# Layer 1's compression pages requested behind the output products of layer 0's attention

## The chip, the core and the metric

The kernel runs on one core of a Trainium2 chip. The metric is device time in microseconds (us); a kernel's time is the median of its runs. Its engines are TensorE (PE, with the weight loads PEld beside it), VectorE (DVE), ScalarE (ACT), GpSimd (POOL) and SyncE (SP). In this kernel SP issues every DMA, and the transfers run on the core's 16 DMA engines.

## The reference, cut to what matters

A decoder step of two layers over 512 prompt tokens and 8 x 4 sample tokens, 1024 channels wide. Each layer normalises its input and multiplies it with one wide weight matrix. The columns feed a state-space branch (S5), an attention branch (NSA) and two sets of merge gates. Both branches are projected to 1024 channels, weighted by the gates, summed, multiplied with an output matrix and added to the layer's input:

```
kc = compress_rows(kv_all[:, :, 0], cmp_pe[0], cmp_w1[0], cmp_w2[0])
vc = compress_rows(kv_all[:, :, 1], cmp_pe[1], cmp_w1[1], cmp_w2[1])
...
b_nsa = (o * jax.nn.silu(z_nsa)) @ lp['w_nsa_out']
m_s5, m_nsa = jnp.split(jax.nn.sigmoid(merge_logits), 2, axis=-1)
out = (m_s5 * b_s5 + m_nsa * b_nsa) @ lp['w_o']
x = x + gate[:, None] * out
```

`compress_rows` turns every block of 64 cached key or value rows into one row by a small two-step network. The cached rows lie in pages of 128 rows, which a page table scatters over a pool. Each layer reads all 128 pages (8 samples x 16 pages) for its compression. That part depends on the cache and on nothing that the previous layer computes.

## The kernel before, in words

Activations are held feature-major: channel blocks of 128 on the partitions, all 544 tokens in the free dimension, worked on in two halves of 256 and 288 tokens. Matrix products in `mm` (line 490) are done in two-part arithmetic: each operand is split into a high and a low part, and three products are summed. A block of output channels times a half of the tokens is 24 matmuls where the contraction is 1024 deep and 12 where it is 512 deep.

**Who sets the order.** The program is written as generators that run against a model clock while the kernel is built (`_Sched.run`, line 252). Each generator emits instructions and yields: `ev` waits until another generator has called `done` with that name, `t` waits some model time, `for` waits for data by the model's clock. A smaller priority number goes first among those that are ready. So the order in which instructions stand in each engine's program, SP's DMA requests too, is fixed when the kernel is built; on the chip every engine works through its own list in that order. Nearly every instruction has the same source line in the profile (the recording helper, line 231), so tiles are told apart by name: `in_cmp` are the compression pages, `mn` and `mt` the spilled gates, `in_nsaow` and `in_wo` the attention's output weights and the layer's output weights, `in_ada_w` the modulation weights. Buffers of the on-chip arena are all called `m`, PSUM banks `bank`.

**Output products of the attention** (in `dense`, lines 1090 to 1122; called the gates' stage below). For each of 8 blocks m of output channels and each token half h: 12 matmuls with `in_nsaow`, then DVE multiplies the sum with the gate `mn`, adds the S5 branch `mt`, and the result is split into two parts. `mn` and `mt` were spilled to DRAM earlier; `gates(m)` (line 1090) reads both back, 272 KB each, into a ring of three buffers, two blocks ahead. Behind the loop stand 8 blocks of products with `in_wo` (the output stage), 24 matmuls a half, beside which the layer's input `in_xT` is loaded and the new activation `x_mid` stored. The weights of all products are requested two blocks of 512 KB ahead of use (`wnext`, line 465).

**Compression of the next layer** (`compress`, line 1612). It is spawned once layer 0's attention is done (event `att`), so it runs beside the gates' stage and the output stage. It loads its first weight (`in_cw`, two halves of 1024 KB) and a position tile (`in_pe`, twice 128 KB), and spawns `loads` (line 1639). `loads` requests 8 chunks of 16 pages, 128 KB a page, four pages at a time, each four behind SP's reading of their page numbers. Layer 1 has two page buffers, so chunk c waits for the products of chunk c - 2 (event `ck`). The products of a chunk are 64 matmul pairs, emitted as 128 matmuls with 64 output rows, ahead of the dense products because their priority number is smaller. Chunks 0 to 4 may come as soon as their pages are there by the model's clock; chunk 5 and later wait until layer 0 is finished (`CMP_LATE`), and the last waits for layer 1's own new rows.

**Modulation of layer 1** (`modulation`, line 531) starts at the same event: 24 blocks of `in_ada_w`, 512 KB each, two at a time, 8 blocks for each of three parts; parts 0 and 1 scale and shift layer 1's input, so `modulate(1)` (line 671) needs them, together with the row norms, before layer 1's first product.

Of the kernel before, what the change touches and what calls it, by code (L numbers as in the profile page):

```python
# [292 lines left out]
def body(ctx: ExitStack, tc: tile.TileContext, A, O):  # L293
# [52 lines left out]
    def t(lat=0.0):  # L346
        return ("t", lat)
# [3 lines left out]
    def ev(*k):  # L351
        return ("ev", k)

    def done(*k):
        S.events[k] = S.ready

    def alloc(n, top=False, keep=0):
        while not mem.fits(n, keep):
            yield "mem", n, keep
        return mem.get(n, top)  # L360
# [150 lines left out]
    def sub(dst_lo, src, hi):  # L511
        dve.tensor_tensor(dst_lo, src, hi.bitcast(F32), op=ALU.subtract)
# [13 lines left out]
    def unlag():  # L526
        while lagged:
            sub(*lagged.pop())
# [226 lines left out]
    def dense(l):  # L755
# [352 lines left out]
        for m2 in range(4):  # L1108
            w = wnext(("nsaow", l, m2))
            for m in (2 * m2, 2 * m2 + 1):  # L1110
# [3 lines left out]
                for h, (a, b) in enumerate(HALVES):  # L1114
# [5 lines left out]
                    split_lag(mh(m, a, b), ml(m, a, b), mt(m, a, b))  # L1120
                    yield t()
        unlag()
        for b in mnb:
            b.free()
        for b in q["ogh"] + [q["ogb"]]:
# [440 lines left out]
    def page_ids(i, n=4):  # L1566
        S.clock.free["sp"] = max(S.clock.free.get("sp", 0.0), S.now) + 0.3 + 0.11 * n
        _, v = nc.values_load_multi_w_load_instructions(
            pt[0:1, i:i + n], engines=[mybir.EngineType.SP], min_val=0, max_val=A["cmp"].shape[0] - 1,
            skip_runtime_bounds_check_because="the page table is clamped to the pool on chip")  # L1570
        return v


    def hidden(hid, b, n, th, xb):

        v = lambda t_: t_[:, 0:2 * n].rearrange("p (n g) -> p g n", g=2)
        dve.scalar_tensor_tensor(hid[:, b, :, 0:n], v(th), 1.0, v(xb), op0=ALU.add, op1=ALU.mult)

    def keys(dst, tmp, cw2, hid, b0, n, w, bank):

        vps = bank[:, 0:w * n].rearrange("p (b n) -> p b n", b=n)
        sh = [P, n, w]
        for j in range(2):
            for g in range(2):
                pe.matmul(bank[g * 64:g * 64 + 64, 0:w * n], cw2[0:64, j, :], hid[0:64, b0:b0 + n, g, 0:w],
                          start=True, stop=True)
            dve.tensor_tensor(dst if j == 0 else tmp, vps,
                              C["kcC" if j == 0 else "kcS"][:, None, 0:w].to_broadcast(sh), op=ALU.mult)
            yield w_
        dve.tensor_tensor(dst, dst, tmp, op=ALU.add)  # L1590
        dve.tensor_scalar(dst, dst, 0.5, None, op0=ALU.mult)

    def products(ck, cw1, npx, bank):
        for d in range(32):
            for ty in range(2):
                pe.matmul(bank[ty * 64:ty * 64 + 64, 0:npx * 4], cw1[ty][:, d, :], ck[:, 0:npx, ty, d, :],
                          start=(d == 0), stop=(d == 31))
            if d % PROD_STEP == PROD_STEP - 1:
                yield t(PROD_GAP)

    def compressed_of(l):

        q = L[l]
        if "kcb" not in q:
            q["kcb"] = None
            kcb = q["kcb"] = yield from alloc(8 * 32 + 2 * P + 16 + 512 + 1 + 128)
            q["kcT"], q["vc"], q["cw2"] = kcb.v(8, 32), kcb.v(2, P, at=256), kcb.v(2, 64, at=1041)
            sp.dma_start(q["cw2"], A["cw2"][l])
            done("kcb", l)
        yield ev("kcb", l)  # L1610

    def compress(l):

        q, keep = L[l], CMP_KEEP if l else 0
        yield from compressed_of(l)
        kcT, vc, cw2, pbias = q["kcT"], q["vc"], q["cw2"], q["kcb"].v(1, at=1040)
        kcbd, vcbd = q["kcbd"], q["vcbd"] = q["kcb"].v(2, 8, at=512), q["kcb"].v(8, 64, p=64, at=528)
        cwb = []
        for _ in range(2):
            cwb.append((yield from alloc(2048, True, keep)))  # L1620
        cw1 = [b.v(32, 64) for b in cwb]

        ckb = []
        for _ in range(CKB[l]):
            ckb.append((yield from alloc((NPG + 5) * 256, True, keep)))
        cks = [b.v(NPG + 5, 2, 32, 4) for b in ckb]
        hb = yield from alloc(512 + 256 + 84 * 2 + 64 + 8 * 2 + 64 * 2, True, keep)
        hid, kt1 = hb.v(8, 2, 32), hb.v(8, 32, at=512)
        xb, th = hb.v(84, at=768), hb.v(84, at=852)
        hnew, kc, kt2, hrep, vcr = (hb.v(1, 2, 32, at=936), hb.v(1, 8, at=1000), hb.v(1, 8, at=1008),  # L1630
                                    hb.v(4, 2, 8, at=1016), hb.v(64, p=64, at=1080))
        for ty in range(2):
            sp.dma_start(cw1[ty], A["cw1"][l, :, ty])
        for ck in cks:
            sp.dma_start(ck[:, NPG].rearrange("p t d c -> p (t d c)"), A["pe4"][l])
        q["cpage"] = cks[(NB - 1) % CKB[l]][:, NPG + 1:NPG + 5]
        done("ckb", l)

        def loads():
            for c in range(NB):  # L1640
                if c >= CKB[l]:
                    yield ev("ck", l, c - CKB[l])
                ck = cks[c % CKB[l]]
                for i in range(0, NPG, 4):
                    for j, v in enumerate(page_ids(NPG * c + i)):
                        sp.dma_start(ck[:, i + j].rearrange("p t d c -> p (t d c)"),
                                     A["cmp"][ds(v, 1), l].rearrange("g p f -> (g p) f"))
                    yield t(PG_LAT)
                yield "for", [], [ck[:, 0:NPG + 1]]
                yield t(CK_LATE)  # L1650
                done("ckl", l, c)
        S.spawn(loads(), 4, "ckload")
        if l > 0:
            yield ev("att", l - 1)
        for c in range(NB):
            if l > 0 and c == CMP_LATE:
                yield ev("x", l - 1)
            last = c == NB - 1
            if last:
                yield ev("cp", l)  # L1660
            yield ev("ckl", l, c)
            npx = NPG + 5 if last else NPG + (c == 0)
            if last:
                yield "for", [], [cks[c % CKB[l]][:, NPG + 1:]]
            yield from products(cks[c % CKB[l]], cw1, npx, B[7])
            done("ck", l, c)
            for b in ([ckb[c % CKB[l]]] if c + CKB[l] >= NB else []) + (cwb if last else []):
                b.free()
            if c == 0:
                dve.tensor_copy(pbias, B[7][:, 64:65])  # L1670
            n = 84 if last else 64
            dve.tensor_scalar(xb[:, 0:n], B[7][:, 0:n], pbias, None, op0=ALU.add)
            act.activation(th[:, 0:n], xb[:, 0:n], AF.Tanh, scale=0.5)
            if last:
                hidden(hnew, 0, 8, th[:, 68:84], xb[:, 68:84])
            hidden(hid, c, 32, th, xb)
        yield w_

        yield from keys(kc, kt2, cw2, hnew, 0, 1, 8, B[7])
        pool.memset(kcbd, 0.0)  # L1680
        for g in range(2):
            dve.tensor_copy(kcbd[g * 64:g * 64 + 64, g, :], kc[g * 64:g * 64 + 64, 0, :])
        dve.tensor_copy(hrep, hnew[:, 0:1, :, 0:8].to_broadcast([P, 4, 2, 8]))
        yield w_
        pe.matmul(B[7][0:64, 0:64], hrep[64:128].rearrange("p r g n -> p (r g n)"), cw2[64:128, 0, :],
                  start=True, stop=True)
        act.activation(vcr, B[7][0:64, 0:64], AF.Copy, scale=0.5)
        dve.tensor_tensor(vcbd, vcr[:, None, :].to_broadcast([64, 8, 64]),
                          C["bd8"][0:64, :, None].to_broadcast([64, 8, 64]), op=ALU.mult)
        done("kcbd", l)  # L1690
        yield w_

        yield from keys(kcT, kt1, cw2, hid, 0, 8, 32, B[7])
        for bh in range(2):
            for b in range(4):
                for g in range(2):
                    pe.matmul(B[7][32 * b:32 * b + 32, g * 64:g * 64 + 64], hid[64:128, 4 * bh + b, g, :],
                              cw2[64:128, 0, :], start=True, stop=True)
            act.activation(vc[:, bh, :], B[7][:, 0:P], AF.Copy, scale=0.5)
            yield w_  # L1700
        hb.free()
        done("cmp", l)
# [385 lines left out]
    def main():  # L2088
# [4 lines left out]
        S.spawn(modulation_first([B[6], B[4]]), 2, "ada0")  # L2093
        S.spawn(modulate(0), 3, "h")
        S.spawn(dense(0), 50, "dense")
        yield ev("modq", 0)
        sp.dma_start(pt, A["page_table"])
# [256 lines left out]
```

## Time and profile before

| | us |
|---|---|
| median of three runs | 1247.3 |
| lowest and highest run | 1238.85, 1257.79 |
| the profiled execution | 1244.75 |
| its span | 1243.0 |
| PE busy in the span | 1142.0 (92%) |
| DVE busy | 780.4 (63%) |
| ACT busy | 481.5 (39%) |

The profiled execution is 1.75 us longer than its span; that much lies around the recorded instructions. Rows of the trace give a start in us from the span's begin, a duration, the engine, the operation with its tiles, a count, and in brackets the engine's idle time before it with the one that ended it. A row merges neighbours of one engine and group, and shows the first one's shape.

### The profile page before, as it was taken

To read this page: it belongs to the slowest core of one execution; us is meant where nothing else is said; L and a number is where in the kernel's file an instruction comes from. 1 tells how busy PE (TensorE), PEld (TensorE's weight loads), DVE (VectorE), ACT (ScalarE), POOL (GpSimd) and SP (SyncE) were. 2 spreads that over 40 slices of the span, in tenths; PEclk is the share of its full clock that TensorE was granted. 3 is DMA by queue.
4 is the path that set the end of the run, shared out by engine and by line. 5 is a ranking of instruction groups with operands and counts; after the bars stand their busy time and mean duration, and the time that the engine had idled before them with its cause. 6 is when DMAs were issued, how large, how long until landed. Compare 5 with 4: busy or idle time off the path is not lost.

```text
span 1243.0 us, 30351 instructions
## 1 busy us (share of the span) xinstructions
PE 1142.0 (92%) x11702; PEld 1037.6 (83%) x11702; DVE 780.4 (63%) x1787; ACT 481.5 (39%) x1130; POOL 154.8 (12%) x335
## 2 busy tenths in 40 slices
PE   4989999999999999887897999979999899999995
PEld 3788999988888888777885899868898788889995
DVE  4766777566666755763336587797665667556854
ACT  4432432333444444432125233244343444454332
POOL 0122261010000000000002033450010000000001
PEclk9999999999999999988998999989999999999997
DMA  9575666657567655349998744545466665733742
GB/s 386 218 225 180 192 181 187 180 176 245 153 187 237 190 165 170 107 165 294 308 308 262 268 162 133 160 135 142 129 213 197 197 194 167 235 104 97 237 131 81
DMA packets 174434, 239.19 MB, mean 192 GB/s; under 512 B 33233, under 2 KB 129618, under 8 KB 172498
## 3 DMA queue, kind: packets, MB, share of 16 engines
q1 hardware_dynamic: 174290, 237.25, 60.2%
q8 instruction: 92, 1.51, 0.5%
q14 instruction: 52, 0.43, 0.1%
HBM read 207.53 MB, written 37.98 MB: 198 GB/s over the span
## 4 chain that ended last, share of the span: by engine, by line
PE 69%; DMA 11%; DVE 7%; ACT 4%; SPq 4%; issue 2%; POOL 0%; DVEq 0%; ACTq 0%; POOLq 0%
PE bank L231 69%; DVE m L231 7%; SPq L231 3%; ACT m L231 3%; DMA m<-in_cmp 2%; DMA m<-in_cw 2%; DMA yd<-m 1%; DMA m<-in_ada_w 1%; DMA m<-kpd 1%; DMA m<-ud 1%; DMA m<-yd 1%; DMA m<-in_s5k 0%; DMA m<-in_wo 0%; ACT L231 0%; DMA gd<-m 0%
## 5 line engine op out<-in xcount | busy, mean ns | idle before, releaser
L231 PE MATMUL bank<-m,m 128*128 128x256 f32 (+13 forms) x10540 | 1048.2, 283 | 62.5 <-DVE m L231 26.6
L231 PEld LDWEIGHTS bank<-m,m 128*128 128x128 f32 (+4 forms) x10540 | 946.5, 168 | 135.5 <-issue 55.4
L231 DVE TENSOR_TENSOR m<-m,m 128x1024 fp32r<-128x1024 f32 (+15 forms) x635 | 386.2, 630 | 156.8 <-ACT m L231 129.6
L231 ACT CAST m<-m 128x1024 fp32r<-128x1024 f32 (+5 forms) x274 | 174.2, 650 | 89.3 <-DVE m L231 62.8
L231 ACT COPY m<-bank 128x512 f32<-128x512 f32 (+7 forms) x258 | 100.1, 400 | 268.0 <-PE bank L231 258.4
L231 ACT ACTIVATE m<-m 128x544 f32<-128x544 f32 (+8 forms) x74 | 34.7, 476 | 186.0 <-DVE m L231 171.8
L231 POOL TENSOR_TENSOR m<-m,m 128x32 f32<-128x32 f32 (+4 forms) x100 | 57.6, 595 | 327.3 <-DMA x_mid<-m 152.8
L231 PE MATMUL bank<-c_k,m 128*128 128x128 f32 (+2 forms) x590 | 88.8, 277 | 5.0 <-DVE m L231 2.8
L231 ACT ACTIVATE m<-bank 128x288 f32<-128x288 f32 (+4 forms) x130 | 50.4, 390 | 104.5 <-PE bank L231 103.8
L231 POOL CAST m<-m 64x128 fp32r<-64x128 f32 x64 | 23.3, 364 | 505.2 <-ACT m L231 426.5
L231 PEld LDWEIGHTS bank<-c_k,m 128*128 128x128 f32 (+1 forms) x590 | 68.0, 145 | 15.0 <-DVE m L231 5.2
L231 ACT ACTIVATE m<-bank,m 128x128 f32<-128x128 f32 (+4 forms) x132 | 67.8, 523 | 14.4 <-DVE m L231 11.4
L231 DVE TENSOR_REDUCE m<-bank 128x1 f32<-128x128 f32 (+4 forms) x132 | 57.3, 474 | 18.6 <-PE bank L231 17.9
L231 DVE COPY m<-bank 128x32 f32<-128x32 f32 (+6 forms) x102 | 39.1, 389 | 46.4 <-ACT m L231 24.7
L231 DVE SCALAR_TENSOR_TENSOR m<-m,bank 128x256 f32<-128x256 f32 x96 | 41.5, 434 | 41.2 <-ACT m L231 25.1
L231 POOL TENSOR_TENSOR m<-m,c_k 128x256 f32<-128x256 f32 (+2 forms) x32 | 36.0, 1126 | 158.8 <-PE bank L231 136.1
L231 DVE TENSOR_SCALAR m<-m,m,m 128x128 f32<-128x128 f32 (+3 forms) x132 | 52.5, 439 | 2.5
L231 DVE SCALAR_TENSOR_TENSOR m<-m,m 128x64 f32<-128x64 f32 (+5 forms) x64 | 28.9, 480 | 18.5 <-ACT m L231 18.0
L231 ACT ACTIVATE m<-m,m 128x512 f32<-128x512 f32 (+2 forms) x24 | 15.9, 662 | 59.9 <-DVE m L231 59.9
L231 DVE SCALAR_TENSOR_TENSOR m<-bank,mod,m 128x256 f32<-128x256 f32 x32 | 15.4, 482 | 34.9 <-PE bank L231 21.3
L231 DVE TENSOR_TENSOR m<-bank,m 64x16 f32<-64x16 f32 (+1 forms) x56 | 19.8, 385 | 24.4 <-PE bank L231 23.4
L231 ACT ACT_TABLE_LOAD x24 | 30.8, 1283 | 7.1 <-DVE m L231 6.0
(59 smaller groups left out, 397.2 us busy)
## 6 DMA issues: line engine op xcount, KB each, us to landing
m<-in_wblk SPq DMA_DIRECT2D x78, 512.0 KB, 4.1
m<-in_cmp SPq DMA_DIRECT2D x256, 128.0 KB, 3.7
m<-in_kvsel SPq DMA_DIRECT2D x256, 128.0 KB, 3.0
m<-in_ada_w SPq DMA_DIRECT2D x32, 512.0 KB, 5.1
m<-in_ada_q SPq DMA_DIRECT2D x8, 1024.0 KB, 14.7
m<-in_wo SPq DMA_DIRECT2D x16, 512.0 KB, 4.8
ms<-m SPq DMA_DIRECT2D x16, 272.0 KB, 3.3
m<-ms SPq DMA_DIRECT2D x16, 272.0 KB, 3.4
```

Source lines behind the costliest of these rows:

```text
L231: return f(*args, **kw)
```

## The change

A new event is set behind the last product and split of the attention's output loop, and the generator that requests the pages waits for layer 0's event before its first request in layer 1. Layer 0's own compression has no such wait. The loads of the compression weights and of the position tile stay where they were, ahead of the wait.

```diff
@@ -1120,6 +1120,7 @@
                     split_lag(mh(m, a, b), ml(m, a, b), mt(m, a, b))
                     yield t()
         unlag()
+        done("nsa", l)
         for b in mnb:
             b.free()
         for b in q["ogh"] + [q["ogb"]]:
@@ -1637,6 +1638,8 @@
         done("ckb", l)
 
         def loads():
+            if l > 0:
+                yield ev("nsa", l - 1)
             for c in range(NB):
                 if c >= CKB[l]:
                     yield ev("ck", l, c - CKB[l])
```

## Rows read from the trace of the kernel before

**Rows 1.** The page: busy time and share of the span, instructions, by engine.
```profile
PE 1142.0 (92%) x11702; PEld 1037.6 (83%) x11702; DVE 780.4 (63%) x1787; ACT 481.5 (39%) x1130; POOL 154.8 (12%) x335
```
**Rows 2.** Stretches: length, busy PE, PEld, DVE, ACT, POOL, clock, DMA share, GB/s.
```profile
537.10:582.70 45.60, 37.26 (x364) 34.84 (x364) 27.39 (x62) 12.21 (x26) 0.00 (x0) 0.87 0.79 264
582.70:664.00 81.30, 72.95 (x1000) 67.15 (x996) 27.89 (x63) 18.76 (x30) 0.00 (x0) 0.99 0.93 304
664.00:698.00 34.00, 26.77 (x386) 23.42 (x385) 18.46 (x53) 12.89 (x34) 6.46 (x22) 0.78 0.81 262
700.00:740.00 40.00, 39.07 (x331) 37.08 (x330) 33.12 (x71) 14.06 (x27) 14.59 (x19) 1.00 0.54 182
```
**Rows 3.** The same view in stretches of 10 us within the gates' stage.
```profile
560.00:570.00 10.00, 5.19 (x24) 5.17 (x24) 2.37 (x6) 0.84 (x2) 0.00 (x0) 0.66 0.81 248
570.00:580.00 10.00, 7.30 (x153) 6.85 (x152) 5.39 (x13) 2.44 (x5) 0.00 (x0) 1.00 1.00 334
```
**Rows 4.** SP's timeline in the gates' stage: start, duration, DMA request.
```profile
551.69 3.66 SPq L231 DMA_DIRECT2D m<-in_cmp  x4
557.54 0.33 SPq L231 DMA_DIRECT2D m<-mn  x1
...
562.40 4.37 SPq L231 DMA_DIRECT2D m<-in_cmp  x8
...
568.74 1.93 SPq L231 DMA_DIRECT2D m<-in_cmp  x4
570.76 0.38 SPq L231 DMA_DIRECT2D m<-mn  x1
```
**Rows 5.** SP's own waits from 551 to 583: us in total, times, longest.
```profile
SPq L231 <- DMA m<-in_cw: 5.8, 2, 3.6
```
**Rows 6.** The chain that ended last, in the gates' stage: start, duration, what.
```profile
549.15 12.37 DMA m<-in_cw
561.53 3.30 DMA m<-mt
...
567.83 5.30 DMA m<-in_wo
```
**Rows 7.** DVE's timeline in the gates' stage.
```profile
564.24 0.42 DVE L231 SCALAR_TENSOR_TENSOR m<-m,bank 128x256 f32<-128x256 f32 x1 [5.65 <-DMA m<-mn]
...
570.46 0.42 DVE L231 SCALAR_TENSOR_TENSOR m<-m,bank 128x256 f32<-128x256 f32 x1 [3.45 <-DMA m<-mn]
...
575.45 0.45 DVE L231 SCALAR_TENSOR_TENSOR m<-m,bank 128x288 f32<-128x288 f32 x1
...
580.38 0.45 DVE L231 SCALAR_TENSOR_TENSOR m<-m,bank 128x288 f32<-128x288 f32 x1 [0.74 <-PE bank L231]
```
**Rows 8.** PE's timeline in the gates' stage.
```profile
564.81 5.37 PE L231 MATMUL bank<-m,m 128*128 128x256 f32 x24 [5.14 <-DVE m L231]
...
574.56 7.21 PE L231 MATMUL bank<-m,m 128*64 128x68 f32 x152 [1.95 <-DMA m<-in_cmp]
```
**Rows 9.** PE's timeline from the output stage's end into layer 1.
```profile
650.91 3.95 PE L231 MATMUL bank<-m,m 128*64 128x64 f32 x128 [0.43 <-DMA m<-in_cmp]
...
654.79 0.71 PE L231 MATMUL bank<-m,ones 128*128 128x128 f32 x4
...
664.05 0.69 PE L231 MATMUL bank<-c_k,m 128*128 128x128 f32 x2
...
685.00 8.80 PE L231 MATMUL bank<-m,m 128*64 128x64 f32 x152 [5.32 <-DMA m<-in_ada_w]
...
761.54 7.95 PE L231 MATMUL bank<-m,m 128*64 128x84 f32 x172
```
**Rows 10.** The tile view of the pages, 470 to 740: duration min/median/max, first and last.
```profile
L231 SPq DMA_DIRECT2D m<-in_cmp x128: 332/333/1791, 551.7 to 697.6; - x128
```
**Rows 11.** DVE's timeline where layer 1's input is modulated.
```profile
665.35 0.28 DVE L231 TENSOR_TENSOR mod<-bank,c_k 128x36 f32<-128x36 f32 x2
...
665.77 0.88 DVE L231 SCALAR_TENSOR_TENSOR m<-m,amul,m 128x256 f32<-128x256 f32 x2
```

## The prediction

> **What bounds the kernel now.** First the page: PE is busy for 92% of the span [rows 1], so over the whole kernel a microsecond is won only where PE idles or runs at its lower clock. Then the table of stretches around the change [rows 2]. The reader is to see that the three stretches from 537.1 to 698 hold 37.3 + 73.0 + 26.8 = 137 us of busy PE in 161 us, so 24 us of PE idle, and that the DMA engines are 79% to 93% busy there; from 700 to 740 it is the other way round, PE 39 of 40 us busy and DMA at 54%. So for 160 us this kernel waits for transfers, and behind them for PE.
>
> Within the gates' stage (537.1 to 582.7) PE idles most from 560 to 580: it is busy 5.2 of the first 10 us, at a mean granted clock of 0.66, and 7.3 of the next 10 [rows 3]. SP's timeline, its waits and the chain tell why [rows 4 to 6]. SP requests four pages at 551.69, then block 5's `mn` only at 557.54, eight pages more, `mn` of block 6 behind them, four pages more, `mn` of block 7 at 570.76. So 4, 12 and 16 pages stand ahead of the three gates. But the pages are not all of it: SP stood 5.8 us, in two waits, for the two halves of `in_cw`, and the chain shows the second landing at 549.15 + 12.37 = 561.5. Each waiting request is the eighth behind the half it waits for (two halves, two position tiles, four pages, then `mn`), so I take it that SP keeps eight requests open. DVE then waits 5.65 us for block 5's `mn` and 3.45 us for block 6's, and PE waits for DVE, because two PSUM banks are all it may run ahead [rows 7, 8].
>
> **The change, part by part.** The two new lines put no instruction and no semaphore wait on the chip; the wait is one of the generator while the program is built. That costs nothing. What moves is all 128 page requests of 128 KB [rows 10], with SP's reading of their page numbers before each four, to behind the stage's last split. On SP they are moved past six gate reloads (blocks 5 to 7), the first `in_wo` blocks, and perhaps a pair of `in_ada_w`. Other engines' work moves with them: each chunk's 128 matmuls on PE (3.95 us for chunk 5 [rows 9]) and four short operations on DVE and ACT, which run beside PE's next work and are put at nothing. No transfer and no matmul is added or taken away.
>
> The sum, by the rate of 334 GB/s that a fully busy DMA reached [rows 3]. Four pages are 0.524 MB, 1.6 us; a gate reload of 272 KB is 0.28 MB, 0.8 us; a block of `in_wo` 1.6 us. `in_cw` is not moved, so block 5's gates still stand behind it. Block 5: without four pages in front, DVE starts at 564.24 - 1.6 = 562.7. Block 6, first half: PE starts 0.6 later as before (563.2) and takes half of 5.37 [rows 8], to 565.9, still at the low clock, which I leave as it is. Its gates follow block 5's `mt`: 562.7 + 3 x 0.8 = 565.1. DVE at 566.0, where it was 570.46: 4.5 us. The first `in_wo`: behind those gates, 565.1 + 1.6 = 566.7, where it landed at 567.83 + 5.30 = 573.1 [rows 6]. Its low part is made on DVE right in front of block 6's second half (575.45 [rows 7]), which so comes 6.4 us earlier, at 569.0. Block 7: two halves of some 1.3 us on DVE behind that (three operations of 0.42 to 0.45), so the last half at 569.0 + 2 x 1.26 = 571.5, where it was 580.38: 8.9 us.
>
> Of these 8.9 us, 3.95 are chunk 0's products, which stood between the blocks (128 of the 152 matmuls at 574.56 [rows 8]) and now come later. That leaves 5.0 us. Where do the 3.95 go? The output stage has PE busy 73 of 81 us, and keeps four chunks (0 to 3 in place of 1 to 4), since their spacing is set by the two buffers. The extra chunk falls behind it, into the stretch from 664 to 698, where PE idles 7.2 of 34 us [rows 2]. If that idle takes it, the gain is 8.9; if the pages that it needs lengthen that stretch, the gain goes and more (a rival, below). I take the value between, full pay for the 3.95, because the rows nearest to it in that stretch show PE waiting on a transfer in front of a chunk (5.32 us for `in_ada_w` [rows 9]). The last chunk has room: its pages are requested by 697.6 and its products stand at 761.54 [rows 9, 10]. What is late next in the gates' stage is block 5's gate behind `in_cw`, of which 3.5 us of idle PE (559.7 to 563.2) remain.
>
> A rule weighed against the row: in the profile a fully busy stretch moved 334 GB/s [rows 3]. The Trainium skill (Perfetto Trace Analysis, Roofline) gives a single core a ceiling of about 435 GB/s over its 16 DMA engines. By that ceiling, an estimate, the four pages ahead of block 5 cost 1.2 us in place of 1.6, the twelve ahead of block 6 3.6 in place of 4.7, and the change would win about a microsecond less; the trace nowhere shows that rate, and the row decides.
>
> The profiled execution took 1244.75, so the sum gives 1239.75. It lies 2.55 below the median of 1247.3, which would give 1242.3. I forecast 1241.
>
> **Rivals.**
> Nothing is won: the transfers end when they ended. If the DMA engines bound the whole 161 us, an order among requests only picks who waits: the output stage begins 9 us earlier and waits that much more for chunk 0 and 1, which are then requested 20 us later. For it: a DMA share of 0.93 through 81 us [rows 2], and PE waiting on pages at 574.56 and 650.91 [rows 8, 9]. Against it: at least the last chunk's 16 pages may pass 698, where DMA falls to 0.54. Time: 1244.75, give or take 2. The Trainium skill (DMA: Bandwidth & Descriptors, Issuing engines are not separate DMA queues) says that all requests run on the same 16 engines and interleave, on which this rival rests; by the shares the trace agrees.
>
> Layer 1 begins earlier too. Layer 1's first modulated tokens start on DVE at 665.77, right behind part 1 of the modulation (665.35), whose transposes on PE stand at 664.05 [rows 9, 11], behind the norm of the second token half. With pages out of the way a pair of `in_ada_w` could fall one place earlier, and DVE could start when the first half's norm is there: PE ends it at 655.5 [rows 9], and with 2 us for ACT's copy that is 657.5, an estimate. That adds 8.3 us: 1239.75 - 8.3 = 1231.5. Against it: the place of those pairs is fixed by the model clock, and DVE is also needed for the last output blocks.
>
> Slower: the pages come to stand where layer 1 starts. Between 664 and 698 the queue carries 32 pages, with modulation weights between them, and PE already waits 5.32 us for `in_ada_w` behind eight pages [rows 9]. One chunk more is 2.1 MB, 8.0 us at the 262 GB/s of that stretch [rows 2]. If PE must wait that out, with a second wait of 5.3 us, the time is 1239.75 + 8.0 + 5.3 = 1253. It decides from the point where more than eight pages stand ahead of a pair of `in_ada_w` that PE's next product waits for. Against it: seven microseconds of PE idle are there to take the products.
>
> That the change doesn't do what it says: the gates stay behind `in_cw`. This is in the sum already for block 5; blocks 6 and 7 are not bound by it, so I give it no case of its own.
>
> **How the numbers follow.** The forecast (4 to 9 us won, 1236 to 1243) gets 0.45, nothing won 0.2, the earlier layer 1 0.15, the slower start 0.2. The predicted time is the forecast's. The range reaches down past 1231.5 and up past 1253, since three quarters of either rival should lie inside: 1228 to 1256. A measurement of this kernel, whose three runs spread over 1.5%, can tell about 2% or 25 us from no change. To be faster by that, the change would have to remove all 24 us of idle PE between 537 and 698: 0.05, out of the third case. Slower by that needs the fourth case and a delay in layer 1 on top of it: 0.06. The rest, 0.89, is within 2%.
>
> **What would show it right or wrong.** In the changed profile, right: no `in_cmp` request before the last gate reload; block 5's `mn` still behind `in_cw`, DVE's wait before it some 4 us, before block 6 about 2 or less; from the stage's first product to block 7's last half 34 us in place of 43; chunk 0 among the output blocks; the stretch up to layer 1's first products shorter by 4 to 9 us, and after it a program as long as before. Wrong: SP waits for something else before the gates; PE waits of more than 5 us for `in_cmp` in the output stage (nothing won); more than 12 us of idle PE between the last output block and layer 1's second product (slower); modulation part 1 ready before the second half's norm (earlier start).

## The result, and the profile after

The changed kernel takes 1233.3 us (median of 16 runs, 1226.64 to 1239.25), the kernel before beside it 1244.64 (16 runs); the ratio on record is 0.9893, 95% interval [0.9872, 0.9913]. It is not the quotient of the two medians, which is 0.9909: by the medians 11 us are won, by the ratio 13 (interval 11 to 16). A second set of runs (run 11 below) gave 0.9876 [0.984, 0.9912], 15 us either way. Forecast was 1241, some 4 to 9 us less than before. The time lies in the range, but below the likeliest case's own 1236 to 1243.

Four stretches take the two profiled executions apart. The gates' stage runs from its first product on PE to DVE's gate of block 7's last half; the output stage from there to the norm of the second token half (DVE's RECIPROCAL of `rsc`); layer 1's start from there to the first rotation product of its first key block (PE, `bank<-m,c_k` 128x256); the rest from there to the end. Ahead of the gates' stage both kernels have one and the same list of PE instructions.

| us | before | after | difference |
|---|---|---|---|
| ahead of the gates' stage | 537.1 | 535.6 | -1.5 |
| gates' stage | 43.3 | 33.0 | -10.3 |
| output stage | 84.2 | 78.7 | -5.5 |
| layer 1's start | 45.0 | 52.6 | +7.6 |
| rest of layer 1 | 533.4 | 526.2 | -7.2 |
| span | 1243.0 | 1226.1 | -16.9 |

These are one execution of each. The first row, the same program, differed from 533.2 to 546.9 over the 14 profiled executions of this study. From the gates' stage on, a profile stands within some 5.5 us of what the medians say: here -15.4 by the table and -11.3 by the medians.

Three stretches of the changed kernel; the first ends some 2 us behind the gates' stage, as it does in [rows 2], and the third is layer 1's start (length, busy PE, PEld, DVE, ACT, POOL, granted clock, DMA share, GB/s), and the first 10 us of [rows 3]:

```profile
535.60:570.80 35.20, 31.99 (x228) 30.79 (x229) 26.72 (x59) 11.84 (x25) 0.00 (x0) 0.88 0.75 270
570.80:647.30 76.50, 72.11 (x1004) 66.26 (x1004) 27.77 (x63) 18.81 (x31) 0.00 (x0) 1.00 0.91 297
647.30:699.90 52.60, 41.85 (x608) 36.16 (x601) 30.34 (x97) 19.50 (x43) 6.08 (x22) 0.87 0.92 307
...
560.00:570.00 10.00, 9.24 (x62) 9.27 (x63) 8.34 (x19) 3.46 (x8) 0.00 (x0) 0.83 0.90 336
```

PE idles 3.2 us in the first stretch, where 8.3 were idle before, and 4.4 in the second, where 8.4 were. From 560 to 570 it is busy 9.2 of 10 us and not 5.2. PE's two largest waits in the output stage of the kernel before are these:

```profile
595.30 6.45 PE L231 MATMUL bank<-m,m 128*64 128x64 f32 x146 [3.29 <-DMA m<-in_cmp]
...
662.92 1.21 PE L231 MATMUL bank<-ones,m 128*128 128x1 f32 x6 [3.04 <-DVE m L231]
```

The two largest after:

```profile
583.33 1.65 PE L231 MATMUL bank<-m,m 128*128 128x256 f32 x12 [1.53 <-DVE m L231]
...
608.86 3.95 PE L231 MATMUL bank<-m,m 128*64 128x64 f32 x128 [1.09 <-DMA m<-in_xT]
```

SP's timeline in the gates' stage, which answers to [rows 4] (start, duration, request):

```profile
547.08 1.26 SPq L231 DMA_DIRECT2D m<-in_cw  x2
548.39 1.71 SPq L231 DMA_DIRECT2D m<-in_pe  x2
550.32 0.47 SPq L231 DMA_DIRECT2D m<-mn  x1
...
552.44 0.32 SPq L231 DMA_DIRECT2D m<-mn  x1
...
556.23 0.33 SPq L231 DMA_DIRECT2D m<-in_wo  x1
558.71 0.32 SPq L231 DMA_DIRECT2D m<-mn  x1
...
569.50 4.38 SPq L231 DMA_DIRECT2D m<-in_cmp  x8
```

The reader is to see that no page stands ahead of the last `mn`, at 558.71, and that the first pages come 11 us behind it, at 569.50. Blocks 5 and 6 have their `mn` requested at 550.32 and 552.44, where it was 557.54 and later.

DVE's timeline of the same stage, with block 5's first half, block 6's two halves and block 7's last half, as in [rows 7]:

```profile
560.19 0.42 DVE L231 SCALAR_TENSOR_TENSOR m<-m,bank 128x256 f32<-128x256 f32 x1 [2.95 <-DMA m<-mn]
...
563.50 0.42 DVE L231 SCALAR_TENSOR_TENSOR m<-m,bank 128x256 f32<-128x256 f32 x1 [0.51 <-PE bank L231]
...
565.94 0.45 DVE L231 SCALAR_TENSOR_TENSOR m<-m,bank 128x288 f32<-128x288 f32 x1
...
568.60 0.46 DVE L231 SCALAR_TENSOR_TENSOR m<-m,bank 128x288 f32<-128x288 f32 x1 [0.15 <-PE bank L231]
```

Block 5 still waits 2.95 us for its `mn`, block 6 no longer for a transfer: PE is its releaser now. The chain of waits says what block 5 waits for:

```profile
550.32 9.77 DMA m<-mn
```

272 KB took 9.77 us from request to landing, behind the 2 MB of `in_cw`. PE's timeline from the end of the output stage (the first row is chunk 3, still in it) into layer 1's start, answering to [rows 9]:

```profile
642.15 3.95 PE L231 MATMUL bank<-m,m 128*64 128x64 f32 x128 [1.01 <-DMA m<-in_cmp]
...
654.13 1.08 PE L231 MATMUL bank<-m,scT 128*32 128x256 f32 x8 [4.58 <-DMA m<-in_ada_w]
...
658.98 8.25 PE L231 MATMUL bank<-m,m 128*64 128x64 f32 x146 [2.27 <-DMA m<-in_cmp]
674.30 6.53 PE L231 MATMUL bank<-m,m 128*64 128x64 f32 x146 [0.75 <-DMA m<-in_cmp]
```

Chunks 4, 5 and 6 (the third of them at 692.98) now stand behind the output stage, where 5 and 6 stood. Before, from 664.6 to 709.6, PE was busy for 37.0 of 45.0 us; now it is 41.9 of 52.6. That is 4.9 us more of busy PE, one chunk's 3.95 and 0.9 on top, and 2.8 more of idle PE.

### The profile page after: what moved, and what is told of

It reads as the page before. It is cut to its first block, busy times and chain, and to the rows that moved or that the text cites. A ratio compares the mean times of both kernels' runs of the same rounds, so it can differ in the third digit from the quotient of the medians.

```text
span 1226.1 us, 30347 instructions
## 1 busy us (share of the span) xinstructions
PE 1138.4 (93%) x11702; PEld 1033.2 (84%) x11702; DVE 780.9 (64%) x1787; ACT 482.4 (39%) x1132; POOL 156.6 (13%) x335
## 4 chain that ended last, share of the span: by engine, by line
PE 68%; DMA 11%; DVE 7%; SPq 4%; issue 4%; ACT 3%; POOL 0%; DVEq 0%; ACTq 0%; POOLq 0%
PE bank L231 68%; DVE m L231 7%; SPq L231 4%; ACT m L231 3%; DMA m<-in_xT 1%; DMA m<-in_cmp 1%; DMA m<-in_kvsel 1%; DMA m<-kpd 1%; DMA m<-yd 1%; DMA m<-in_ada_w 1%; DMA yd<-m 1%; DMA m<-mn 1%; DMA m<-in_cw 1%; ACT L231 1%; SPq L1569 0%
## 5 line engine op out<-in xcount | busy, mean ns | idle before, releaser
L231 PE MATMUL bank<-m,m 128*128 128x256 f32 (+11 forms) x10540 | 1045.6, 281 | 51.9 <-DVE m L231 26.2
L231 PEld LDWEIGHTS bank<-m,m 128*128 128x128 f32 (+2 forms) x10540 | 943.5, 167 | 127.3 <-issue 48.7
L231 DVE TENSOR_TENSOR m<-m,m 128x1024 fp32r<-128x1024 f32 (+16 forms) x635 | 391.0, 638 | 157.2 <-ACT m L231 124.7
L231 ACT CAST m<-m 128x1024 fp32r<-128x1024 f32 (+7 forms) x274 | 174.5, 650 | 82.2 <-DVE m L231 54.9
L231 ACT COPY m<-bank 128x512 f32<-128x512 f32 (+6 forms) x258 | 99.5, 400 | 253.2 <-PE bank L231 242.3
L231 ACT ACTIVATE m<-m 128x64 f32<-128x64 f32 (+7 forms) x74 | 34.8, 476 | 180.4 <-DVE m L231 171.2
L231 ACT ACTIVATE m<-bank 128x256 f32<-128x256 f32 (+5 forms) x130 | 50.4, 389 | 109.4 <-PE bank L231 105.9
L231 DVE COPY m<-bank 128x32 f32<-128x32 f32 (+6 forms) x102 | 39.1, 390 | 48.1 <-PE bank L231 34.2
L231 DVE TENSOR_SCALAR m<-m,m,m 128x128 f32<-128x128 f32 (+4 forms) x132 | 52.6, 440 | 2.5
L231 ACT ACT_TABLE_LOAD x26 | 33.4, 1283 | 18.1 <-DVE m L231 17.0
L231 ACT ACTIVATE m<-m,m 128x512 f32<-128x512 f32 (+2 forms) x24 | 15.9, 662 | 52.7 <-DVE m L231 52.7
L231 PE MATMUL bank<-m,scT 128*32 128x256 f32 (+1 forms) x320 | 30.2, 487 | 6.2 <-DMA m<-in_ada_w 6.2
## 6 DMA issues: line engine op xcount, KB each, us to landing
m<-in_ada_q SPq DMA_DIRECT2D x8, 1024.0 KB, 14.7
```

Of the source, the lines that this page charges most:

```text
L231: return f(*args, **kw)
```

## The experiments

All stages by the definitions above, in us; "head" is the sum of the three stages in front of the rest. Stages are read from one profile of each; a ratio is to the kernel before, run in the same set.

| run | gates | output | start | head | rest | ratio, 95% interval |
|---|---|---|---|---|---|---|
| before | 43.3 | 84.2 | 45.0 | 172.5 | 533.4 | 1 |
| after | 33.0 | 78.7 | 52.6 | 164.3 | 526.2 | 0.9893 [0.9872, 0.9913] |
| 1, products held | 41.2 | 83.4 | 52.3 | 176.9 | 538.0 | 1.0062 [1.0033, 1.0091] |
| 2, pages behind the last reload request | 33.5 | 79.8 | 58.0 | 171.3 | 525.9 | 0.9913 [0.9876, 0.9949] |
| 3, pages behind output block 1 | 33.2 | 83.1 | 52.9 | 169.1 | 540.7 | 1.0024 [0.9997, 1.0051] |
| 4, S5 later | 33.6 | 79.9 | 56.7 | 170.3 | 551.5 | 1.0134 [1.0097, 1.0172] |
| 5, after, then before's order | 33.8 | 78.0 | 52.9 | 164.8 | 531.5 | 0.9975 [0.9943, 1.0006] |
| 6, before, then after's order | 43.5 | 83.4 | 45.4 | 172.3 | 540.9 | 1.0084 [1.0056, 1.0113] |
| 7, weights behind too | 29.4 | 88.0 | 51.7 | 169.1 | 521.9 | 0.9921 [0.9892, 0.9951] |
| 8, as 1, before's order | 41.8 | 86.4 | 52.7 | 180.9 | 531.0 | 1.0042 [1.0013, 1.007] |
| 9, weights between | 28.6 | 78.8 | 53.8 | 161.2 | 628.6 | 1.0652 [1.0611, 1.0692] |
| 10, the same, own order | 28.4 | 82.7 | 54.2 | 165.2 | 549.7 | 1.0039 [1.0018, 1.0061] |
| 11, after again | 34.2 | 78.1 | 54.2 | 166.5 | 525.7 | 0.9876 [0.984, 0.9912] |
| 12, as 9, after's order | 29.4 | 82.1 | 53.4 | 164.9 | 527.1 | 0.9864 [0.9827, 0.9902] |

**Which part of the change shortens the head: 1 to 3.** Run 1 leaves the pages where they were and only holds chunk 0's products back (the event is set where the change sets it):

```diff
@@ compress, of the kernel before
             yield ev("att", l - 1)
+            yield ev("nsa", l - 1)
```

> The kernel before, with one edit: the pages are requested where they were, but layer 1's first chunk of products (chunk 0) waits until the gates' stage has ended. If the gain comes from the reloads being requested ahead of the pages, nothing of it is here: DVE's two waits for mn stay near 5.7 and 3.5 us, the gates' stage (first product to block 7's last half, 43.3 us before, 33.0 in the changed kernel) shortens only by what chunk 0's products took, to 39 to 41 us, and the whole time is 0.997 to 1.002 of before. If instead it is the products of one chunk leaving the stretch ahead of layer 1 that wins, wherever the reloads stand, the time falls as in the changed kernel, to 0.987 to 0.992.

DVE's two waits for `mn` are still there:

```profile
563.20 0.42 DVE L231 SCALAR_TENSOR_TENSOR m<-m,bank 128x256 f32<-128x256 f32 x1 [4.81 <-DMA m<-mn]
...
570.45 0.42 DVE L231 SCALAR_TENSOR_TENSOR m<-m,bank 128x256 f32<-128x256 f32 x1 [4.49 <-DMA m<-mn]
```

The gates' stage lost only 2.1 us of its 43.3 though 3.95 us of products had left it, and layer 1's start got 7.2 longer; the ratio, 1.0062, lies above both expectations. So holding the products wins nothing by itself and costs the start 7 us; the other 8 us of the gates' stage come with the reloads being requested first.

Run 2 keeps the change but sets the event as soon as the last reload has been requested, run 3 sets it only behind output block 1:

```diff
@@ dense, of the changed kernel (run 2)
+                if m == 5:
+                    done("nsa", l)
                 for h, (a, b) in enumerate(HALVES):
...
         unlag()
-        done("nsa", l)
```

> The changed kernel, but the pages wait only until the last of the reloads has been requested, not until the last product. The reloads stand ahead of all pages as in the changed kernel; the pages come a little earlier. If the reloads make the gain, the gates' stage is 33 to 35 us and the time 0.987 to 0.993 of before. A rival: about half of the changed kernel's gain comes from layer 1, where its program has the state-space branch earlier among the dense products. In this kernel's program that branch's last tile stands behind 1500 dense matmuls counted from the gates' stage, against 1362 before and 1308 in the changed kernel; by the rival the rest of the kernel from layer 1's first key block on is then no shorter than before (533 us), and the time is 0.994 to 0.998.

```diff
@@ dense, of the changed kernel (run 3)
         unlag()
-        done("nsa", l)
...
                 square_acc(acc, xn(m), m)
+            if (m, h) == (1, 1):
+                done("nsa", l)
```

> The changed kernel, but the pages wait further, until two of the eight output blocks are done. The gates' stage should be as in the changed kernel (33 us) by every theory. If deferring pages and products is what wins, the output stage loses one more chunk (3.95 us) and the time falls on, to 0.984 to 0.988. If the reloads' order wins, nothing more is to be had: 0.988 to 0.993, with the output stage shorter by a chunk and the stretch up to layer 1's first key block longer by a chunk or more. The state-space branch's last tile stands at 1314 dense matmuls, as in the changed kernel (1308), so the layer 1 rival expects the changed kernel's time as well.

Both have the gates' stage of the changed kernel (33.5 and 33.2): once the reloads stand ahead of the pages, how far behind them the pages come doesn't matter to it. (Chunk 0's products have left the stage in both, so no run shows the reloads' order without that.) It does matter behind the stage. In run 2 the output stage takes three chunks only, and the start is 58.0. Its time is as expected, and its rest of 525.9 is against the rival named there, which had 533. Run 3's head leaves chunk 6's 4 us to the rest, so it is 173 us on equal terms, no better than before's 172.5; its ratio, 1.0024, missed every expectation, by a rest of 540.7.

**The rest of layer 1: 4, 5, 6 and 8.** The 7.2 us at the far end lie where the change has no instruction. Two causes were open: what the new head hands on (the S5 branch, for one, starts 23.0 us ahead of the rest and not 14.0), or the order of layer 1's program, which the model clock lays anew when anything in front of it moves. Run 4 delays S5:

```diff
@@ dense, of the changed kernel
             yield ev("h", l + 1)
+            yield t(9.0)
             S.spawn(s5(l + 1), S5_PRIO, "s5")
```

> The changed kernel with one edit behind it: layer 1's state-space branch is started 9 us later by the model clock (its last tile then stands at 1398 dense matmuls in place of 1308; before 1362). Up to layer 1's first products the program is the changed kernel's. If the branch's earlier place is what shortens layer 1 (from 533 to 526 us from the first key block to the end), 5 to 9 us are lost and the time is 0.993 to 0.998 of before. If the gain is all ahead of layer 1, the time stays at 0.987 to 0.991.

The rest took 551.5 us, 25 more than the changed kernel's, and the ratio, 1.0134, is beyond both expectations. In its profile S5 starts 20.7 us ahead of the rest, not much later than the 23.0. Since the delay also laid the order anew, this alone doesn't tell the two causes apart. Runs 5 and 6 do. In them the generators of one kernel are emitted by its own clock up to layer 1's first key block, and behind it in an order recorded from the other kernel; by operation, tiles and shape the last 4595 of PE's 11702 instructions are then the other kernel's:

```diff
+            led = self.follow(free) if SWAP_AT in self.events else None
-            ready = [t for t in free if t[1] <= self.now]
+            ready = [led] if led else [t for t in free if t[1] <= self.now]
...
-            if others > FAIR or pe.lags(self.now):
+            if not led and (others > FAIR or pe.lags(self.now)):
```

> The program is that of the changed kernel up to layer 1's first key block; from there on the instructions are emitted in the order in which the kernel before emits them. Nothing is left out. Theory A (the 7.2 us by which layer 1's rest got shorter come from the order of its program, which the change laid anew): the rest takes about 533 us as in the kernel before, the head keeps its 8.2 us, so the time is 8 us below the kernel before, ratio 0.991 to 0.996. Theory B (they come from what the new head hands on, such as an earlier S5 branch): the rest stays at 526, ratio 0.986 to 0.990.

> The reverse: the kernel before up to layer 1's first key block, then the changed kernel's order. Nothing is left out. Theory A (program order): the head as in the kernel before (43, 84 and 45 us), the rest about 526 in place of 533, so 7 us won without any of the change's own gain, ratio 0.992 to 0.996. Theory B (what the head hands on): rest at 533, ratio 0.998 to 1.002.

Run 5: rest 531.5, as theory A has it; the order before costs its time behind the new head too. Its ratio, 0.9975, is above what A gave, so the head's gain is nearer 3 us by the ratio (interval -0.7 to 7.1; 4.7 by the medians) than the 7.7 that the heads of the two profiles differ by. Run 6: neither theory. The changed kernel's order behind the old head takes 540.9, longer than both. Nearly all of the difference between before and after lies between the first key block and SP's first request of `in_kvsel`, the selected rows: 208.6 us before, 202.5 after, and 324.8 against 323.7 behind it. PE's timeline with its waits shows why. In the kernel before:

```profile
815.55 1.30 PE L231 MATMUL bank<-m,c_k 128*128 128x288 f32 x2 [2.27 <-POOL m L231]
835.39 3.96 PE L231 MATMUL bank<-m,m 128*128 128x256 f32 x28 [5.11 <-DVE m L231]
```

In run 5, the new head with before's order:

```profile
807.10 0.72 PE L231 MATMUL bank<-m,c_k 128*128 128x288 f32 x2 [2.30 <-POOL m L231]
827.07 3.96 PE L231 MATMUL bank<-m,m 128*128 128x256 f32 x28 [5.95 <-DVE m L231]
```

In run 6, the old head with the changed kernel's order:

```profile
716.50 0.33 PE L231 MATMUL bank<-c_k,m 128*128 128x128 f32 x1 [0.98 <-DVE m L231]
719.81 0.90 PE L231 MATMUL bank<-c_k,m 128*128 128x128 f32 x3 [2.99 <-DVE m L231]
...
866.80 7.84 PE L231 MATMUL bank<-m,m 128*64 128x80 f32 x64 [5.98 <-DMA m<-ud]
```

And DVE's timeline in the kernel before, ahead of the second of its two waits (a row merges neighbours and shows the first one's shape):

```profile
817.93 5.33 DVE L231 TENSOR_TENSOR m<-m,m 128x576 f32<-128x576 f32 x9
...
824.63 6.33 DVE L231 TENSOR_TENSOR m<-m,m 128x576 f32<-128x576 f32 x10
...
831.51 3.50 DVE L231 TENSOR_TENSOR m<-m,m 128x64 f32<-128x64 f32 x8
834.92 0.42 DVE L231 SCALAR_TENSOR_TENSOR m<-m,bank 128x256 f32<-128x256 f32 x1
```

In before's order DVE works through some 30 operations, the rows of 128x576 and 128x64, and the emptying of a PSUM bank (834.92) stands behind them; PE's next wide product starts 0.05 us after it is done. The wait is there with either head, 126 us behind the first key block in one and 125 in the other, and once more in run 8 (5.96 us). No run takes this block out of the order by itself: that it costs the 5 to 6 us is read from these rows, not tested. The stretch of 25 us around the wait, and the next one, as the table of stretches of the kernel before has them: DVE is busy for 23.3 of 25 us, PE for 18.1, and the granted clock is 0.89 and 0.91.

```profile
809.64:834.64 25.00, 18.11 (x148) 16.67 (x147) 23.31 (x43) 13.64 (x24) 11.98 (x23) 0.89 0.46 151
834.64:859.64 25.00, 23.42 (x203) 22.08 (x204) 18.98 (x45) 8.68 (x23) 3.55 (x8) 0.91 0.28 80
```

The changed kernel's order has no such block; the largest waits on its PE timeline from 700 to 902 are these two:

```profile
768.45 8.68 PE L231 MATMUL bank<-m,m 128*128 128x256 f32 x66 [2.55 <-DVE m L231]
...
810.60 2.87 PE L231 MATMUL bank<-m,m 128*128 128x256 f32 x22 [1.86 <-DVE m L231]
```

But behind the old head it waits more than before's order does: 3.97 us at its beginning, and 5.98 us for `ud`, a tile of the S5 branch on its way through DRAM, where before's order waits 1.76 us (1.89 in run 5). That fits the lead of S5 (its first 128x16 operation on DVE ahead of the first key block): with leads of 23.2, 23.0, 22.5 and 20.3 us (run 7, after, run 11, run 12) the changed kernel's order takes 521.9, 526.2, 525.7 and 527.1, with run 6's 14.3 it takes 540.9. Before's order takes 533.4, 531.5 and 531.0 with leads of 14.0, 23.3 and 14.7. So it looks as if one order has a fixed stall and needs no lead, and the other has no stall and needs the lead. The lead is read from these eight profiles and wasn't varied by itself. It doesn't decide across orders: runs 1 to 4 and 10, each with an order of its own, have leads of 14.6, 19.9, 24.0, 20.7 and 20.3 us and rests of 538.0, 525.9, 540.7, 551.5 and 549.7.

> The first experiment again (pages requested early as before, only chunk 0's products held behind the output loop), with layer 1's order behind its first key block taken from the kernel before. Nothing is left out. Its own rest was 538 us in place of 533. If that was the program laid anew, it is 533 to 534 now, and what stays is the head: 0 to 4 us longer than before, ratio 1.000 to 1.003. If holding the products costs layer 1 something, the rest stays at 538 and the ratio at 1.006.

Run 8 is run 1 with before's order behind the first key block. The rest is 531.0 and not 538.0, so run 1's longer rest was the order too. The head is 8.4 us over before's and not 0 to 4; with run 1's 4.4 that is the spread of one program, and the ratio, 1.0042, between the two expectations. Holding the products alone makes the kernel slower, by the head.

**In search of a version that beats both: 7 and 9 to 12.** Block 5 still waited for `in_cw`. Run 7 puts `in_cw` and `in_pe` behind the same event; its order behind the first key block is the changed kernel's (a wait marked `again` is left out of the recorded order):

```diff
@@ compress, of the changed kernel
+        if l > 0:
+            yield "ev", ("nsa", l - 1), "again"
         for ty in range(2):
             sp.dma_start(cw1[ty], A["cw1"][l, :, ty])
```

> The change, and with it the compression weight (in_cw, two halves of 1 MiB) and the position tile also requested behind the last split; layer 1's order behind its first key block is that of the changed kernel. If block 5's gates wait for in_cw and for nothing else, DVE's 2.95 us wait in front of block 5 goes, and the gates' stage takes 30 to 31 us in place of 33.0. If this is kept, the ratio is 0.984 to 0.989, a little under the changed kernel's 0.989; if the compression then starts too late (rival), PE waits for in_cw or in_cmp in the output stage and behind it, and the stretch up to the first key block gives the 2 to 3 us back: 0.988 to 0.993.

The gates' stage fell to 29.4, a little under what was expected, and DVE doesn't wait for block 5's `mn` any more, so block 5 did wait for `in_cw` alone. The output stage gave it back and more: 88.0 us. The ratio, 0.9921, lies in the rival's range, but for another reason: not the compression is late, but the layer's own input. SP's timeline of run 7:

```profile
582.95 9.16 SPq L231 DMA_DIRECT2D m<-in_cmp  x8
592.17 0.42 SPq L231 DMA_DIRECT2D m<-in_xT  x1
```

And its DVE timeline:

```profile
595.28 0.88 DVE L231 SCALAR_TENSOR_TENSOR m<-bank,mod,m 128x256 f32<-128x256 f32 x2 [8.08 <-DMA m<-in_xT]
```

The eight pages behind `in_cw` kept SP for 9.16 us, where eight took 4.38 in the changed kernel, and `in_xT` of the next output block stood behind them. SP's waits from 576 to 593 give the reason (us in total, times, longest):

```profile
SPq L231 <- DMA m<-in_cw: 4.1, 2, 2.1
```

Runs 9, 10 and 12 therefore request the weights between the last gate and the pages:

```diff
@@ dense and compress, of the changed kernel
+                if m == 5:
+                    done("nw", l)
                 for h, (a, b) in enumerate(HALVES):
...
+        if l > 0:
+            yield ev("nw", l - 1)
         for ty in range(2):
             sp.dma_start(cw1[ty], A["cw1"][l, :, ty])
```

> The change, with the compression weight and the position tile requested once the last gate reload is requested (between the gates and the pages) and the pages behind the last split as in the changed kernel; order of layer 1's rest from the changed kernel. Nothing is left out. If the 9 us that the seventh experiment lost in the output stage come from the residual input in_xT queueing behind the pages requested at once with the weights: gates' stage 29.5 to 31, output stage back at 78 to 80, ratio 0.983 to 0.988. If the 2 MB of weights simply have to be moved somewhere in this stretch, and PE waits for something else instead: output stage 81 or more, ratio 0.988 to 0.993.

> The same edit with the order that its own model clock lays for layer 1. Head as in the run beside it within 1 us. If layer 1's rest depends on the order as the fifth and sixth experiments showed, it lies anywhere from 520 to 545 us here, and the two kernels differ by that alone; if it does not, they agree within 2 us.

> The changed kernel itself, on the same chip as the two beside it: ratio 0.987 to 0.992 as before. Gates' stage 33, output stage 78.5, layer 1's start 52.5, rest 526 us, each within 1.5 us, if stages repeat from profile to profile.

> The ninth experiment again. There the last part of layer 1's order was not that of the changed kernel: the compression's last step was emitted behind the wide products, and the attention ran alone at the end. Here the last 3900 of PE's products stand in the changed kernel's order. Head as in the ninth run: gates' stage 28 to 29, output stage 78 to 83, layer 1's start 53 to 54.5 us. If that head feeds the changed kernel's order in time: rest 520 to 527 and ratio 0.980 to 0.988, below the changed kernel. If its later compression (in_cmp waits of 3.6 and 6.1 us in layer 1's start) makes the rest wait, as the kernel before's head did in the sixth experiment: rest 530 to 541, ratio 0.990 to 1.003.

The order behind the first key block is to be the changed kernel's in runs 9 and 12 and its own model clock's in run 10; run 11 is the changed kernel once more.

Run 9's order of the rest was not the intended one (its last compression step, and with it the attention, came behind the wide products); its time tells nothing of the edit, only what an order can cost: 628.6 us for work that takes 526. Run 10, with the order that its own model clock lays, took 549.7 there, beyond the top of its expected range, and its head is 4 us longer than run 9's, where 1 us was expected. Run 11 came out as expected but for layer 1's start, 54.2 us. Run 12 has the order meant for run 9: rest 527.1, ratio 0.9864, which isn't told apart from the changed kernel's 0.9876 (run 11) or 0.9893. The gates' stage is 28 to 29 us in all three, some 4 to 6 less than in the changed kernel, but the output stage takes 78.8, 82.7 and 82.1: the heads come to 161, 165 and 165, against 164 to 166. So two runs of three speak for the second theory of run 9 (the 2 MB have to move somewhere). No version here beats the changed kernel for sure.

## Why the prediction was right, and where it was not

**The gates' stage: right, a little small.** Counted from the stage's first product, block 5 came 2.5 us earlier (1.6 predicted), block 6's first half 5.5 (4.5), its second half 8.0 (6.4), block 7's last half 10.3 (8.9). The mechanism is the one worked out: pages out of the queue, block 5 still behind `in_cw` with DVE waiting 2.95 us (some 4 said), the others bound by PE; 33.0 us in place of 43 where 34 was named. Part of the surplus is the spread of a single profile: in runs 5 and 11, with the same head, DVE waits 3.68 and 4.08 us for block 5, and on average over these three profiles, against the two of the old head (before and run 6), the four figures are 2.0, 5.2, 7.5 and 9.7. So the first term (four pages at 1.6 us) isn't shown to be mis-sized. The prediction left the clock low; it was 0.83 from 560 to 570 where it had been 0.66, so part of what remains may be the clock's.

That SP keeps eight requests open is borne out, as a property of this program: in each of the 14 traces SP's 1046 requests take eight semaphores in turn, and no request starts before the one eight ahead of it has landed (in the 908 cases whose landing is recorded). In the changed kernel the two that SP holds back for the halves of `in_cw` are `in_wo` (556.23) and block 7's `mn` (558.71).

**"The output stage keeps four chunks": right, and its length wrong.** Four chunks stand in it as said, but it lost 5.5 us, which no term had. The two largest waits of before's stretch are gone: 3.29 us for the pages of chunk 1 and 3.04 us for DVE at the second half's norm; the largest that remain are 1.53 and 1.09. "Nothing is won", the rival by which this stage would wait 9 us more, fell here.

**The extra chunk behind it: right in kind, too small.** 3.95 us were charged for chunk 0's products. Layer 1's start got 7.6 longer: 4.9 of busy and 2.8 of idle PE, with 4.58 us of waiting for `in_ada_w` and 2.27 for pages. That is the mechanism of the slower rival, at about half of its price (13.3), and run 1 shows it without the rest of the change (7.2). The two misses nearly cancel, by luck: -5.5 in the output stage, and 3.7 more than charged in the start.

**"After it a program as long as before": wrong.** This is the step that failed. The rest of layer 1 is 7.2 us shorter in the profile, because its order was laid anew: run 5, the same head with the old order, has 531.5 us there and a ratio of 0.9975 against 0.9893 and 0.9876. Between these ratios lie 10 to 12 us of the 13 to 15 that the changed kernel wins by them (by the medians 7 to 10 of 11 to 15); its head, the only thing that was forecast, is worth 3 by the ratio (interval -0.7 to 7.1), or 8 by the profiles. The forecast of 4 to 9 us for the head is borne out by the profiles and not decided by the timed runs. The new order wins only together with the new head: behind the old one it takes 540.9 us (run 6). That the time fell below the likeliest case's range is the order's doing, which had no rival and no price in the prediction; that it stayed within the whole range owes something to luck, since the rests of other orders differ by up to 25 us from the changed kernel's (run 4). An order can as well cost: three of the edits (runs 3, 4 and 10) kept the short gates' stage and lost more in the rest than they had won.

**"Layer 1 begins earlier":** its condition did not come. Part 1 of the modulation was ready at 649.65, 2.4 us behind the second half's norm (647.3), as it had been 0.8 us behind it before.

```profile
647.26 0.18 DVE L231 RECIPROCAL rsc<-rsc 128x3 f32<-128x3 f32 x1 [4.24 <-ACT rsc L231]
...
649.65 0.30 DVE L231 TENSOR_TENSOR mod<-bank,c_k 128x36 f32<-128x36 f32 x2 [0.60 <-PE bank L231]
```

**"The gates stay behind `in_cw`"** held for block 5 alone, as said; run 7 prices it at 3.6 us of the gates' stage.

The sum went by 334 GB/s [rows 3] and called a higher rate one that the trace nowhere shows. That is a wrong reading: the trace of the kernel before shows 424 GB/s at the kernel's start and 395 within the gates' stage itself, ahead of the stretch that was read (columns as in [rows 2]):

```profile
10.00:20.00 10.00, 7.85 (x46) 4.04 (x46) 3.59 (x12) 3.39 (x7) 0.00 (x0) 1.00 1.01 424
551.00:561.00 10.00, 8.17 (x71) 7.15 (x70) 5.75 (x13) 2.63 (x5) 0.00 (x0) 1.00 1.03 395
```

The changed kernel has 410 there:

```profile
552.00:562.00 10.00, 6.79 (x57) 5.80 (x56) 4.83 (x11) 2.19 (x4) 0.00 (x0) 0.95 1.03 410
```

The Trainium skill (Perfetto Trace Analysis, Roofline) puts a single core's ceiling at about 435 GB/s; the trace bears it out, with 424 just below it.

## What to carry to other kernels

Requests that nobody waits for soon should stand behind those that the running stage waits for; the gain is counted at the end of the next two stages, since one stage's 10 us came back in part (7.6 us) where the moved work landed. Where a scheduler lays the program while it is built, moving a request by a few microseconds lays everything behind it anew; that can be worth more than the edit itself, here 521.9 to 551.5 us for the rest of layer 1, leaving out the run whose order was not the intended one. Before a gain is put down to an edit, hold the order behind it fixed, as runs 5 and 6 do, and take no single profile's difference of 5 us for real.

## What was not expected of the hardware

The same list of PE instructions ahead of the gates' stage took 533.2 to 546.9 us in 14 profiled executions, while a head of one program repeated within 2.2 us (164.3, 164.8 and 166.5: after, runs 5 and 11) or within 4.0 (176.9 and 180.9: runs 1 and 8).

Eight pages of 128 KB kept SP for 9.16 us behind 2.25 MB of weights and position tiles and for 4.38 us without. Of the 9.16, SP stood 4.1 waiting for the two halves of `in_cw` to land, because each request takes the semaphore of the one eight ahead of it. So in this program a large load costs the requests behind it twice: SP is held up, and the transfer takes longer (272 KB took 9.77 us from request to landing behind 2 MB).
